# Feed-forward heads of a decoder trunk: evacuations ahead of the block sums, sums grouped, a third tile on the un-normed stream

## The chip, the cores and the metric

One Trainium2 chip, one of its cores. The metric is the device time of one execution in microseconds (us), the median of several; a profile of one execution stands beside it. Times inside a profile count from the start of its span.

## The reference, cut to what matters

The program is a decoder trunk of two layers on 512 tokens of width 1024, in fp32. Each layer has two feed-forward half steps, and this is all that the change touches:

```python
def rms_norm(x, g):
    y = x32 * lax.rsqrt(jnp.mean(x32 * x32, axis=-1, keepdims=True) + EPS)
    return (y * g.astype(jnp.float32)).astype(x.dtype)

def swiglu(h, w_gate, w_up, w_down):
    return (jax.nn.silu(h @ w_gate) * (h @ w_up)) @ w_down
...
    for i in range(DEPTH):
        x = x + 0.5 * swiglu(rms_norm(x, g[0]), ffn_w_gate[i, 0], ffn_w_up[i, 0], ffn_w_down[i, 0])
        ...                                   # mixers: gMLP and HGRN2 in layer 0, latent attention in layer 1
        x = x + 0.5 * swiglu(rms_norm(x, g[2]), ffn_w_gate[i, 1], ffn_w_up[i, 1], ffn_w_down[i, 1])
        x = x + per_layer_embedding(rms_norm(x, g[3]), p[i], ple_w_gate[i], ple_w_proj[i], g[4])
```

`w_gate` and `w_up` are 1024 x 2816, `w_down` is 2816 x 1024. The norm is a factor per token, so (x · gain) @ W, scaled per token afterwards, is the same as rms_norm(x) @ W.

## The kernel before, in words

Activations lie transposed: 1024 features are 8 tiles of 128 partitions x 512 tokens, the 2816 hidden features are 22 such tiles. Every fp32 operand is split in two: a high part, a cast on ScalarE (ACT, L115 in `cut`), and a low part, a subtract on VectorE (DVE, L116). A product is three matmuls, high·high, high·low and low·high (L127 to L129 in `mm3`). `weights` loads a block of weights (a `raw` tile), and splits it into a `wh` and a `wl` tile, five of each in rotation; `feat` multiplies one hidden tile of gate or up from eight feature tiles, 24 matmuls of 128x512; a down tile of `down(0, 4)` is 12 such matmuls.

`ffn` runs four times: two layers, two half steps each. Each run begins with a head. Its order in the source:

- The first two hidden tiles (gate and up each) are multiplied from `x`, the split stream with the gain but without the norm. Their `evacuate` scales them on DVE by `rb`, the norm's factor spread over the partitions (L384, L387), takes silu on ACT, multiplies (L388) and cuts.
- `rb` comes from `norm_of` and `along`: four small matmuls (L223, the spread) and a copy on ACT (L237). In the first and third run (arguments `first` and `tail`) the norm is made while the first two tiles run, and comes late; in the second and fourth it is ready early.
- `quarters` (L321 to L324) makes block differences of the next weights on DVE.
- `normed` (L275 on DVE, then a cut) makes the normed stream, eight tiles `ns`, once `rb` is there.
- The hidden tiles `m` = 2 and 3, called third and fourth here, are multiplied from the normed stream (`rest`).
- `combine` makes sums and differences of halves of the normed tiles (128x256 adds, L289), four of each, and cuts all eight: the operands of a seven-product block scheme.
- Then the third and fourth tile are evacuated: silu from the accumulator on ACT (L382), multiply (L388), cut.
- `down(0, 4)` multiplies the first four hidden tiles into the stream; four of its eight steps stand here, each 12 matmuls and one DVE row that adds to `x` (L448).
- Then the rest: `gate(p)` and `up(p)` call `seven`, seven products (L348 to L350) of 12 matmuls of 128x256 each, weights split as before, with further down steps between.

The engines' orders aren't written by hand. A scheduler merges the source into one order for each engine when the program is built; at run time each engine goes through its own list, and stands where a row waits. Accumulators are named `ps` and `pb`, split tiles `big`, scratch `tmp`.

Of the kernel before, what the change touches and what calls it, by code (L numbers as in the profile page):

```python
# [9 lines left out]
F32R = mybir.dt.float32r  # L10
# [8 lines left out]
KD = DM // P  # L19
# [34 lines left out]
class Net:  # L54
# [228 lines left out]
    def combine(self, ns):  # L283
        V = self.nc.vector
        lo, hi = slice(0, T // 2), slice(T // 2, T)
        self.xc = [{} for _ in range(KD // 2)]

        def add(o, x, y, op):
            V.tensor_tensor(out=o, in0=x, in1=y, op=op)  # L289

        for i, d in enumerate(self.xc):
            d["x11"] = self.halves(ns[2 * i][1])[0]
            d["x12"], d["x22"] = self.halves(ns[2 * i + 1][1])
        sums = []
        for i, d in enumerate(self.xc):
            e, o = ns[2 * i][0], ns[2 * i + 1][0]
            s = self.big()
            add(s[:, lo], e[:, hi], o[:, hi], ALU.add)
            add(s[:, hi], s[:, lo], e[:, lo], ALU.subtract)
            c = self.big(F32R), self.big(F32R)  # L300
            self.cut(*c, s)
            d["s1"], d["s2"] = self.halves(c)
            sums.append(s)
        for i, d in enumerate(self.xc):
            e, o = ns[2 * i][0], ns[2 * i + 1][0]
            s = self.big()
            add(s[:, lo], e[:, lo], e[:, hi], ALU.subtract)
            add(s[:, hi], o[:, lo], sums[i][:, hi], ALU.subtract)
            c = self.big(F32R), self.big(F32R)
            self.cut(*c, s)  # L310
            d["s3"], d["s4"] = self.halves(c)

    def quarters(self, src):
# [57 lines left out]
    def ffn(self, i, f, g_next, embedding=False, tail=None, first=None):  # L371
# [3 lines left out]
        x = self.xs  # L375
        w = a["w_g0"][i, f]
        act = []

        def evacuate(gps, ups, rb=None):
            t, u = self.tmp(), ups  # L380
            if rb is None:
                nc.scalar.activation(out=t, in_=gps, func=AF.Silu)  # L382
            else:
                V.tensor_tensor(out=t, in0=gps, in1=rb, op=ALU.mult)  # L384
                nc.scalar.activation(out=t, in_=t, func=AF.Silu)
                u = self.tmp()
                V.tensor_tensor(out=u, in0=ups, in1=rb, op=ALU.mult)  # L387
            V.tensor_tensor(out=t, in0=u, in1=t, op=ALU.mult)  # L388
            h, l = self.big(F32R), self.big(F32R)
            self.cut(h, l, t)  # L390
            act.append((h, l))
# [29 lines left out]
        if rb is None:  # L421
            rb = self.along(r)
# [2 lines left out]
        evacuate(*pss[:2], rb)  # L425
        evacuate(*pss[2:], rb)
        xn = [c for _, c in ns]
        rest = [self.feat(w[m, n], xn) for m in (2, 3) for n in range(2)]
        self.combine(ns)
        ns = None  # L430
        evacuate(*rest[:2])
        evacuate(*rest[2:])
        gates = {}

        def gate(p):
# [40 lines left out]
        for m in range(3):  # L476
# [3 lines left out]
            for k in range(4):  # L480
                s = slice(k * P, (k + 1) * P)
                self.mm3(pss[m], wh[:, s], wl[:, s], *act[k0 + k], k == 0, False)
        for m in range(3):
            wh, wl, _ = next(early[m])
            for k in range(2):
                s = slice(k * P, (k + 1) * P)
# [927 lines left out]
```

## Time and profile before

| | us |
|---|---|
| median of three runs | 2053.76 |
| lowest and highest | 2048.27, 2054.41 |
| the profiled execution, its own time | 2051.09 |
| its span | 2049.2 |

| engine | busy share of the span |
|---|---|
| PE (TensorE matmuls) | 96% |
| DVE | 76% |
| ACT | 48% |

The chain of work that ended last goes through PE for 84% of the span and through DVE for 10%. The mean granted clock of PE over the span is 0.984 of full. The span is the time from the first to the last instruction that the profile shows; the execution's own time is 1.9 longer.

How to read it: an engine takes its rows in order, so a wait of one row holds all rows behind it. For a stretch the windows view gives each engine's busy time and the granted clock; the timeline gives the starts, and in square brackets the idle time before a row and what ended it. Matmuls are pipelined, so their starts, not their durations, tell the pace. The rows that count stand further below.

### The profile page before, as it was taken

What the parts mean: (1) busy time and instruction counts of PE and PEld (TensorE: products, weight loads), DVE (VectorE), ACT (ScalarE), POOL (GpSimd) and SP (SyncE); (2) the same over time, 40 slices, a digit from 0 to 9 for tenths busy, and PEclk for the clock granted to TensorE, in tenths of its full rate; (3) what the DMA queues carried; (4) which work ended last, traced back from release to release, by engine and by line L of the source; (5) the groups of instructions that cost most, each with busy time, mean ns of one, the idle gap of its engine ahead of it and who ended that gap; (6) DMA issues with size and microseconds to landing.
All of it is one profiled execution on the core that took longest, in us unless ns stands there. A gap on an engine that the chain in (4) does not pass through costs nothing.

```text
span 2049.2 us, 32390 instructions
## 1 busy us (share of the span) xinstructions
PE 1969.0 (96%) x12324; PEld 1761.1 (86%) x12324; DVE 1550.6 (76%) x3047; ACT 992.1 (48%) x1852; POOL 86.4 (4%) x94
## 2 busy tenths in 40 slices
PE   8899999989999999999987999999899999999997
PEld 6799999868887999998976999998777879999996
DVE  7787777677468778777788877775876688778776
ACT  5454445423344554455544544454654455444463
POOL 0000000220000000000000000001420000000001
PEclk9999999999999999999999999999999999999999
DMA  5233333322122233334322333333111222333342
GB/s 174 71 100 103 114 93 104 93 83 70 44 92 94 83 113 93 100 118 124 118 88 67 104 100 116 95 104 97 48 33 35 88 86 91 113 93 98 114 139 88
DMA packets 68571, 193.68 MB, mean 95 GB/s; under 512 B 7744, under 2 KB 10304, under 8 KB 68416
## 3 DMA queue, kind: packets, MB, share of 16 engines
q1 hardware_dynamic: 68416, 191.63, 29.9%
q8 instruction: 96, 1.57, 0.3%
q14 instruction: 59, 0.48, 0.1%
HBM read 189.50 MB, written 2.10 MB: 93 GB/s over the span
## 4 chain that ended last, share of the span: by engine, by line
PE 84%; DVE 10%; DMA 2%; ACT 2%; issue 1%; POOL 0%; SPq 0%; ACTq 0%; DVEq 0%; POOLq 0%
PE ps L127 13%; PE ps L128 13%; PE ps L129 13%; PE ps L349 6%; PE ps L348 6%; PE ps L350 6%; PE pb L348 5%; PE pb L349 5%; PE pb L350 5%; DMA raw<-in_w_gs 2%; DVE wl L116 1%; DVE big L116 1%; PE ps L165 1%; PE ps L166 1%; PE ps L167 1%
## 5 line engine op out<-in xcount | busy, mean ns | idle before, releaser
L115 ACT CAST wh<-raw 128x512 fp32r<-128x512 f32 (+2 forms) x637 | 384.9, 607 | 494.6 <-PE ps L128 167.0
L116 DVE TENSOR_TENSOR wl<-raw,wh 128x512 fp32r<-128x512 f32 (+1 forms) x605 | 406.3, 676 | 201.1 <-ACT wh L115 196.2
L127 PE MATMUL ps<-big,wh 128*128 128x512 f32 (+2 forms) x1376 | 519.2, 382 | 36.6 <-ACT big L115 28.0
L129 PE MATMUL ps<-big,wl 128*128 128x512 f32 (+2 forms) x1376 | 521.3, 380 | 10.2 <-DVE wl L116 10.0
L128 PE MATMUL ps<-big,wh 128*128 128x512 f32 (+2 forms) x1376 | 521.9, 380 | 0.5 <-DVE big L116 0.3
L127 PEld LDWEIGHTS ps<-big,wh 128*128 128x128 f32 (+1 forms) x1376 | 261.1, 190 | 84.9 <-ACT big L115 33.0
L350 PE MATMUL ps<-big,wl 128*128 128x256 f32 x1152 | 326.0, 283 | 0.0
L349 PE MATMUL ps<-big,wh 128*128 128x256 f32 x1152 | 326.0, 283 | 0.0
L348 PE MATMUL ps<-big,wh 128*128 128x256 f32 x1152 | 325.7, 283 | 0.0
L129 PEld LDWEIGHTS ps<-big,wl 128*128 128x128 f32 (+1 forms) x1376 | 261.5, 190 | 59.0 <-DVE wl L116 13.6
L128 PEld LDWEIGHTS ps<-big,wh 128*128 128x128 f32 (+1 forms) x1376 | 262.1, 190 | 49.2 <-DVE big L116 3.3
L115 ACT CAST wh<-tmp 128x512 fp32r<-128x512 f32 x288 | 178.6, 620 | 245.7 <-PE ps L128 118.3
L348 PE MATMUL pb<-big,wh 128*128 128x256 f32 x864 | 246.9, 286 | 1.4 <-DVE big L353 1.1
L349 PE MATMUL pb<-big,wh 128*128 128x256 f32 x864 | 244.4, 283 | 0.0
L350 PE MATMUL pb<-big,wl 128*128 128x256 f32 x864 | 244.3, 283 | 0.0
L348 PEld LDWEIGHTS ps<-big,wh 128*128 128x128 f32 x1152 | 220.9, 192 | 2.7
L349 PEld LDWEIGHTS ps<-big,wh 128*128 128x128 f32 x1152 | 220.9, 192 | 2.7
L350 PEld LDWEIGHTS ps<-big,wl 128*128 128x128 f32 x1152 | 220.9, 192 | 0.0
L116 DVE TENSOR_TENSOR wl<-tmp,wh 128x512 fp32r<-128x512 f32 x288 | 194.6, 684 | 11.0 <-ACT wh L115 9.8
L348 PEld LDWEIGHTS pb<-big,wh 128*128 128x128 f32 x864 | 164.9, 191 | 13.8 <-DVE big L353 13.0
L349 PEld LDWEIGHTS pb<-big,wh 128*128 128x128 f32 x864 | 165.2, 191 | 0.0
L350 PEld LDWEIGHTS pb<-big,wl 128*128 128x128 f32 x864 | 165.0, 191 | 0.0
(271 smaller groups left out, 2593.9 us busy)
## 6 DMA issues: line engine op xcount, KB each, us to landing
raw<-in_w_gs SPq DMA_DIRECT2D x144, 512.0 KB, 4.3
raw<-in_w_dn SPq DMA_DIRECT2D x128, 256.0 KB, 2.7
raw<-in_w_pg SPq DMA_DIRECT2D x28, 512.0 KB, 3.3
raw<-in_w_dn SPq DMA_DIRECT2D x32, 384.0 KB, 3.4
raw<-in_w_ei SPq DMA_DIRECT2D x24, 512.0 KB, 3.6
raw<-in_w_g SPq DMA_DIRECT2D x20, 512.0 KB, 3.5
raw<-in_w_g SPq DMA_DIRECT2D x24, 256.0 KB, 2.7
raw<-in_w_eo SPq DMA_DIRECT2D x8, 512.0 KB, 3.2
```

What stands on the lines that cost most here:

```text
L115: self.nc.scalar.copy(out=h, in_=src)
L116: (eng or self.nc.vector).tensor_tensor(out=l, in0=src, in1=h.bitcast(F32), op=ALU.subtract)
L127: mm(ps, wh, xh, start=first, stop=False)
L128: mm(ps, wh, xl, start=False, stop=False)
L129: mm(ps, wl, xh, start=False, stop=last)
L165: mm(o, x[0][:, t], wh, start=first, stop=False)
L166: mm(o, x[0][:, t], wl, start=False, stop=False)
L167: mm(o, x[1][:, t], wh, start=False, stop=last)
L348: mm(banks[bank], h[:, s], xh, start=new and i == 0, stop=False, **kw)
L349: mm(banks[bank], h[:, s], xl, start=False, stop=False, **kw)
L350: mm(banks[bank], l[:, s], xh, start=False, stop=i == KD // 2 - 1, **kw)
```

## The change

In `ffn`, the tiles `m` = 2 and 3 are each evacuated right behind their products in the source, ahead of `combine` instead of behind it. In the first and third run (`first` or `tail`) the third tile (`m` = 2) is multiplied from the un-normed `x` and scaled by `rb` in its evacuation, like the first two; the fourth, and both in the other two runs, stay on the normed stream. In `combine` all four sums come first, then the four cuts of sums with the differences between them, then the four cuts of differences; before, each sum and each difference was cut at once. Lines behind the edits shift by three or four: L384, L387 and L388 are L387, L390 and L391, and L448 is L452.

```diff
--- before.py
+++ after.py
@@ -292,22 +292,25 @@
             d["x11"] = self.halves(ns[2 * i][1])[0]
             d["x12"], d["x22"] = self.halves(ns[2 * i + 1][1])
         sums = []
-        for i, d in enumerate(self.xc):
+        for i in range(KD // 2):
             e, o = ns[2 * i][0], ns[2 * i + 1][0]
             s = self.big()
             add(s[:, lo], e[:, hi], o[:, hi], ALU.add)
             add(s[:, hi], s[:, lo], e[:, lo], ALU.subtract)
-            c = self.big(F32R), self.big(F32R)
-            self.cut(*c, s)
-            d["s1"], d["s2"] = self.halves(c)
             sums.append(s)
+        diffs = []
         for i, d in enumerate(self.xc):
             e, o = ns[2 * i][0], ns[2 * i + 1][0]
+            c = self.big(F32R), self.big(F32R)
+            self.cut(*c, sums[i])
+            d["s1"], d["s2"] = self.halves(c)
             s = self.big()
             add(s[:, lo], e[:, lo], e[:, hi], ALU.subtract)
             add(s[:, hi], o[:, lo], sums[i][:, hi], ALU.subtract)
+            diffs.append(s)
+        for i, d in enumerate(self.xc):
             c = self.big(F32R), self.big(F32R)
-            self.cut(*c, s)
+            self.cut(*c, diffs[i])
             d["s3"], d["s4"] = self.halves(c)
 
     def quarters(self, src):
@@ -425,11 +428,12 @@
         evacuate(*pss[:2], rb)
         evacuate(*pss[2:], rb)
         xn = [c for _, c in ns]
-        rest = [self.feat(w[m, n], xn) for m in (2, 3) for n in range(2)]
+        for m in (2, 3):
+
+            late = m == 2 and (first or tail)
+            evacuate(*[self.feat(w[m, n], x if late else xn) for n in range(2)], rb if late else None)
         self.combine(ns)
         ns = None
-        evacuate(*rest[:2])
-        evacuate(*rest[2:])
         gates = {}
 
         def gate(p):
```

The number of matmuls stays as it was. DVE has 3035 rows where it had 3029 in the merged lists. The lists of POOL and of the sync queue, which issues the loads, are unchanged. In the lists below `big`, `tmp`, `wl` and `wh` are tiles as above, and the numbers in names tell tiles apart; those of one program aren't those of the other.

PE in the first run's head, behind the norm's spread, before: the third tile's first matmuls take the first normed tile (`big_339`, `big_340`).

```order
L129 MATMUL pb_95<-big_272,wl_225 128x512
L223 MATMUL pb_320<-cst,ty_294 128x128 x4
L127 MATMUL ps_406<-big_339,wh_409 128x512
L127 MATMUL ps_441<-big_339,wh_444 128x512
L127 MATMUL ps_476<-big_339,wh_479 128x512
L128 MATMUL ps_406<-big_340,wh_409 128x512
L129 MATMUL ps_406<-big_339,wl_410 128x512
```

The same place now, with the un-normed tiles `big_88`, `big_89` and `big_133`.

```order
L129 MATMUL pb_95<-big_272,wl_225 128x512
L223 MATMUL pb_320<-cst,ty_294 128x128 x4
L127 MATMUL ps_406<-big_88,wh_409 128x512
L128 MATMUL ps_406<-big_89,wh_409 128x512
L129 MATMUL ps_406<-big_88,wl_410 128x512
L127 MATMUL ps_406<-big_133,wh_409 128x512
```

Behind the spread stand now matmuls on tiles that were there for the first two tiles already.

DVE in the same head, from the last splits of `combine` to the adds of the down steps, before: the low parts of the third and fourth activation (`big_606`, `big_613`) stand behind the last split (`big_599`).

```order
L116 TENSOR_TENSOR big_592<-big_588,big_591 128x512
L289 TENSOR_TENSOR big_595<-big_374 128x256
L289 TENSOR_TENSOR big_595<-big_380,big_567 128x256
L116 TENSOR_TENSOR big_599<-big_595,big_598 128x512
L116 TENSOR_TENSOR big_606<-tmp_602,big_605 128x512
L116 TENSOR_TENSOR big_613<-tmp_609,big_612 128x512
L323 TENSOR_TENSOR tmp_850<-raw_844,tmp_848 128x512
L324 TENSOR_TENSOR tmp_849<-raw_844,raw_843 128x512
L448 SCALAR_TENSOR_TENSOR x<-ps_616,x 128x512
```

DVE now, where the fourth tile is multiplied (L391): its low part (`big_560`) stands ahead of the first add of `combine`.

```order
L391 TENSOR_TENSOR tmp_556<-ps_521,tmp_556 128x512
L116 TENSOR_TENSOR big_483<-tmp_476,big_482 128x512
L116 TENSOR_TENSOR wl_683<-raw_680,wh_682 128x512
L116 TENSOR_TENSOR big_560<-tmp_556,big_559 128x512
L289 TENSOR_TENSOR big_563<-big_338,big_344 128x256
L289 TENSOR_TENSOR big_566<-big_350,big_356 128x256
```

And DVE at the end of `combine` now: the first product's low weight part (`wl_703`, of `raw_326`) stands behind the last split (`big_616`); before, that part stood amid the sums, ahead of the last sum's split.

```order
L116 TENSOR_TENSOR big_604<-big_579,big_603 128x512
L452 SCALAR_TENSOR_TENSOR x<-ps_639,x 128x512
L116 TENSOR_TENSOR big_608<-big_586,big_607 128x512
L452 SCALAR_TENSOR_TENSOR x<-ps_659,x 128x512
L116 TENSOR_TENSOR big_612<-big_593,big_611 128x512
L452 SCALAR_TENSOR_TENSOR x<-ps_679,x 128x512
L116 TENSOR_TENSOR big_616<-big_600,big_615 128x512
L116 TENSOR_TENSOR wl_703<-raw_326,wh_702 128x512
```

What has moved is the whole `combine`, with the adds to `x` strewn in: from ahead of the activations' cuts to behind them, and from behind the first product's weight part to ahead of it. ACT's list follows: its casts of differences (`big_607`, `big_611`, `big_615`) stand behind the cast of a product's weights (`wh_771`).

```order
L115 CAST big_603<-big_579 128x512
L115 CAST wh_771<-tmp_332 128x512
L115 CAST big_607<-big_586 128x512
L115 CAST big_611<-big_593 128x512
L115 CAST big_615<-big_600 128x512
```

In the third run's head the scheduler also moves some 37 small DVE rows of the latent attention's angles (L954 to L996), which stood in the head, to places among the seven-product blocks behind it.

## Rows read from the trace of the kernel before

**Rows 1.** The page, first part: busy us, share of the span, instructions.

```profile
PE 1969.0 (96%) x12324; PEld 1761.1 (86%) x12324; DVE 1550.6 (76%) x3047; ACT 992.1 (48%) x1852; POOL 86.4 (4%) x94
```

**Rows 2.** PE's waits: us in total, times, longest.

```profile
PE ps L127 <- ACT big L115: 28.0, 6, 10.1
```

**Rows 3.** Timeline of PE, first head: start, us, instruction, [idle before, its releaser].

```profile
31.77 0.60 PE L223 MATMUL pb<-cst,ty 128*128 128x128 f32 x4
35.20 0.99 PE L127 MATMUL ps<-big,wh 128*128 128x512 f32 x3 [2.83 <-ACT big L115]
...
59.66 0.39 PE L128 MATMUL ps<-big,wh 128*128 128x512 f32 x1
...
64.64 0.39 PE L129 MATMUL ps<-big,wl 128*128 128x512 f32 x1
73.82 0.80 PE L127 MATMUL ps<-big,wh 128*128 128x512 f32 x1 [8.79 <-ACT big L115]
...
82.64 0.28 PE L348 MATMUL ps<-big,wh 128*128 128x256 f32 x1
82.76 0.28 PE L349 MATMUL ps<-big,wh 128*128 128x256 f32 x1
```

**Rows 4.** Windows: us, busy of PE, PEld, DVE, ACT, POOL, PEclk, DMA share, GB/s.

```profile
28.00:83.00 55.00, 43.20 (x174) 33.78 (x172) 44.53 (x91) 26.09 (x44) 0.00 (x0) 0.88 0.20 58
35.00:40.00 5.00, 4.64 (x13) 3.41 (x14) 5.00 (x10) 3.74 (x6) 0.00 (x0) 0.66 0.16 48
83.00:386.00 303.00, 302.76 (x2039) 279.23 (x2038) 228.29 (x394) 150.68 (x280) 5.17 (x4) 1.00 0.34 103
```

**Rows 5.** Timeline of DVE in the first head.

```profile
33.75 0.75 DVE L275 SCALAR_TENSOR_TENSOR big<-x,par,rb 128x512 f32<-128x512 f32 x1
34.41 0.69 DVE L384 TENSOR_TENSOR tmp<-ps,rb 128x512 f32<-128x512 f32 x1
...
65.10 0.69 DVE L116 TENSOR_TENSOR big<-big,big 128x512 fp32r<-128x512 f32 x1 [0.69 <-ACT big L115]
65.71 0.42 DVE L289 TENSOR_TENSOR big<-big 128x256 f32<-128x256 f32 x1
66.04 0.42 DVE L289 TENSOR_TENSOR big<-big,big 128x256 f32<-128x256 f32 x1
67.14 0.69 DVE L116 TENSOR_TENSOR big<-big,big 128x512 fp32r<-128x512 f32 x1 [0.68 <-ACT big L115]
```

**Rows 6.** Timeline of PE in the third head.

```profile
1060.99 0.98 PE L127 MATMUL ps<-big,wh 128*128 128x512 f32 x3 [2.11 <-ACT big L115]
...
1089.68 0.39 PE L129 MATMUL ps<-big,wl 128*128 128x512 f32 x1
1100.13 1.22 PE L127 MATMUL ps<-big,wh 128*128 128x512 f32 x2 [10.06 <-ACT big L115]
...
1107.77 0.28 PE L348 MATMUL ps<-big,wh 128*128 128x256 f32 x1
```

**Rows 7.** Windows of the third head and of the products behind it.

```profile
1060.00:1108.00 48.00, 36.58 (x146) 28.12 (x147) 46.45 (x113) 22.06 (x39) 0.00 (x0) 0.89 0.16 50
1108.00:1430.00 322.00, 321.74 (x2125) 294.51 (x2124) 240.06 (x418) 161.41 (x298) 5.83 (x6) 1.00 0.33 101
```

**Rows 8.** Timeline of DVE in the third head.

```profile
1059.53 0.75 DVE L275 SCALAR_TENSOR_TENSOR big<-x,par,rb 128x512 f32<-128x512 f32 x1 [2.03 <-ACT rb L237]
...
1094.56 0.28 DVE L980 SCALAR_TENSOR_TENSOR sm<-sm,sm 128x128 f32<-128x128 f32 x1
1094.76 0.28 DVE L978 SCALAR_TENSOR_TENSOR sm<-sm,sm 128x128 f32<-128x128 f32 x1
```

**Rows 9.** Timeline of PE in the second head.

```profile
662.42 0.39 PE L129 MATMUL ps<-big,wl 128*128 128x512 f32 x1
664.80 0.97 PE L127 MATMUL ps<-big,wh 128*128 128x512 f32 x3 [2.00 <-ACT big L115]
...
670.40 0.28 PE L348 MATMUL ps<-big,wh 128*128 128x256 f32 x1
```

## The prediction

> **What bounds the kernel now.** I read the page's first part, then what the tensor engine waits for, then its order of time in the four feed-forward heads, then the same stretches by engine. PE is busy for 96% of the span and DVE for 76% [rows 1], so time can come only out of PE's idle stretches and out of stretches at the lower clock. The list of PE's waits has one entry far above the rest: first-term matmuls (L127) waiting for a high part that ACT cut into a `big` tile, 28.0 us in six waits, the longest 10.1 [rows 2]. Those six lie in the heads of the four feed-forward blocks, where the change is; I call the heads 1 to 4 in order of time. In head 1 PE ends the norm's spread at about 32.1, starts the third tile at 35.20 after an idle of 2.83, ends the first half of the first down products at 64.64 + 0.23 = 64.87 (22 steps from 59.66 to 64.64 make 0.227 a matmul), and stands 8.79 until 73.82 [rows 3]. Head 3 has the same shape: 2.11 before 1060.99 and 10.06 before 1100.13 [rows 6]. Heads 2 and 4, whose norm is early, have one wait each: 2.00 before 664.80 in head 2 [rows 9], and in head 4 what remains of the 28.0, 2.2. After the heads PE has no room left: 302.76 busy of 303 between 83 and 386, with DVE at 228.29 [rows 4]. A head that ends sooner therefore moves everything behind it by as much.
>
> What DVE does in the long wait is the point. From 65.10 on each split of a sum (L116) starts after 0.69 of waiting for ACT, and the next split comes 2.04 later: add, cast on ACT, subtract, one block at a time [rows 5]. The cut of the third tile's activation stands behind all of that on DVE and ACT. It is order, not data, that makes PE wait.
>
> The clock is part of the bill. Between 35 and 40, after the idle of 2.83, the granted clock is 0.66 of full, a mix of its two levels, 2.4 and 1.2 GHz; that is 5.0 x 0.34 = 1.7 lost [rows 4]; the 24 matmuls from 73.82 to 82.64 take 8.82 where 24 x 0.227 = 5.45 would do, so 3.4 are lost after the idle of 8.79 [rows 3]. In head 3 the like stretch takes 1107.77 - 1100.13 = 7.64, 2.2 lost [rows 6]. In head 2 it takes 670.40 - 664.80 = 5.60: an idle of 2.00 lost nothing [rows 9].
>
> **The change part by part.** Prices of DVE rows are distances between starts of queued rows, which are less than durations: a 128x512 subtract 0.61 (65.10 to 65.71), `normed` 0.66 (33.75 to 34.41), a 128x256 add 0.33 (65.71 to 66.04) [rows 5]. I use 0.60 for every 128x512 row but `normed`, 0.67 and 0.34.
>
> *Third tile from the un-normed stream, heads 1 and 3.* Its 48 matmuls need no norm, so they start behind the spread, at 32.1 instead of 35.20, at full clock, and end at 32.1 + 48 x 0.227 = 43.0. The fourth tile still needs the normed stream, and DVE makes that: the 32 rows from the first `normed` at 33.75 to the last normed low part, now with the third tile's two scaling products and one multiply among them, are 8 x 0.67 + 23 x 0.60 + 0.2 = 19.4, so 53.2. Eight matmuls stand behind that last part, 1.8, with some 0.2 to start: the fourth tile ends at 55.2. Before it ended at 64.87 - 24 x 0.227 = 59.4 [rows 3]. That is 4.2 gained. Four products are added on DVE in the whole program (two in each late head); they lie inside the 19.4.
>
> *Evacuations ahead of the combine, sums grouped.* Before, the first product started 82.64 - 59.4 = 23.2 after the fourth tile. Now PE goes on without a wait through all 48 down matmuls, to 55.2 + 10.9 = 66.1, since the last activation's parts stand ahead of the combine. What is late next is the first product's low weight part, which the order puts behind the whole combine on DVE. From the end of the fourth tile: 0.2 to start, one multiply, two cuts and a down-weight cut (4 x 0.60 = 2.4), eight adds of the sums (2.7), then eight splits, eight adds of the differences and four adds to x (4.8 + 2.7 + 2.4 = 9.9), then that low part (0.7): 15.9, so 71.1. Two product matmuls of 0.12 (82.64 to 82.76 [rows 3]) run before it is needed, so PE waits from 66.3 to 71.1, 4.8, and the product stands as if started at 70.9. Gain against 82.64: 11.7.
>
> The new idle of 4.8 lies between 2.83, which cost 1.7, and 8.79 and 10.06, which cost 3.4 and 2.2. I take the mean of the three, 2.4, with 0 and 3.4 as ends. Head 1: -11.7 + 2.4 = **-9.3**. The Trainium skill (TensorE: Matmul & The Clock Gate, section HAM oscillation) holds that a long enough idle of PE throws it back to its lower clock until it has worked again; by that rule the new idle is not free and the sum stays, and this trace agrees at 2.83 and above, and shows no fall at 2.00.
>
> *Head 3.* The spread is pushed behind four matmuls of the third tile, so the first `normed` row comes 4 x 0.227 = 0.9 later than 1059.53 [rows 8]; 32 rows of the same kinds, 19.4, bring the last normed part to 1079.8 and the fourth tile's end to 1081.8, instead of 1089.91 - 5.45 = 1084.5 [rows 6]. The cuts of the first activations are still queued on DVE then: eight of 0.60 and two small ones, 5.1, to 1084.9. After that 2.7 + 9.9 + 0.7 give 1098.2 for the low part of the second product, which here is the late one (the first one's stands ahead of the combine). The first product stands as if started at 1098.2 - 0.24 - 1.44 = 1096.5 (1.44 is twelve matmuls of 0.12) instead of 1107.77: -11.3, and with 2.4 for the clock **-8.9**. Some 37 small rows of the odd layer's angles, 0.20 each between starts [rows 8], 7.6 together, stood largely in this head (113 DVE rows against 91 in head 1 [rows 4, 7]) and now stand among the products behind it. There DVE is busy for 240.06 of 322 [rows 7], so I take **+0.5**, from 0 to 2.
>
> *Heads 2 and 4.* No third-tile change; the wait of 2.00 goes. But DVE now has nothing from about 647 to 657, since the combine stands behind the fourth tile's multiply, which needs PE. From the fourth tile's end at 662.65 - 5.45 = 657.2: multiply, one weight cut, one activation cut with 0.2 to start 2.0, adds of the sums 2.7, seven splits, eight adds and four adds to x 4.2 + 2.7 + 2.4 = 9.3, the second product's low part 0.7: 671.9. PE is there at 657.2 + 10.9 + 1.44 + 0.24 = 669.8 and waits 2.1. The first product stands as if at 670.2 instead of 670.40: **-0.2** each. An idle of 2.1 is nearest to the 2.00 that cost no clock; the other end is 1.7 each.
>
> Matmuls are as many as before. The orders of the sync queue and of POOL are unchanged, so no transfer moves past another.
>
> **How the numbers follow.** -9.3 - 8.9 + 0.5 - 0.4 = -18.1. Against the profiled execution, 2051.1, that is 2033.0; its median of three stands 2.7 higher, and I put the forecast a little up, at **2034**. About 0.3%, 6 us, is what a measurement of this kernel tells from no change.
>
> **Rivals.**
> No clock is lost in the new idles: -11.7 - 11.3 - 0.4 + 0.5 = -22.9, 2028 against the profiled execution and 2031 against the median. For it: some idles fall without a loss (2.00). Against: 2.83 lost 1.7. Chance 0.13.
> ACT holds half the splits. In ACT's order the casts of the differences stand behind casts of product weights, which wait for a weight tile that PE frees only at the end of each down product. By my times the last of them comes at 66.1, about 1 before DVE asks for the parts behind it; if PE is later than that, four splits a head fall back to the old 2.04 instead of 0.60 + 0.68 = 1.28, 3.0 a head, 12 in all: 2046. Chance 0.13, about half of it within 0.3%.
> The third tile isn't early, because its weights' cuts hold it: the fourth tile then ends at 59.4 and only the second gain is left, 11.7 - 4.2 - 2.4 = 5.1 in heads 1 and 3: 2041. Against: those weights' rows stand ahead of the first `normed` on DVE. Chance 0.05.
> Slower: all eight splits of every head stay a ping-pong at 2.04. That is 8 x 0.76 = 6.1 a head, 24 in four, and it lengthens the idles of heads 2 and 4 past 2.83, where each loses 1.7 of clock: 2034 + 24 + 3 = 2061. It decides from 18.1 / 32 = 0.57 a split on. Against it: four finished sums lie ready for ACT before DVE needs the first cast. Chance 0.05. The Trainium skill (VectorE: DVE Perf Modes, section The DRAIN you can't avoid) found a chain of DVE copies equally long with and without a semaphore after each; by that rule regrouping brings nothing, which is this rival. The trace doesn't follow it here: the 0.68 is a wait for another engine.
>
> The forecast itself has 0.64: it holds from 2028 to 2040. The range, **2027 to 2043**, takes in the gain without a clock loss and the late third tile, and leaves out most of the ACT case and the slower one. Faster by over 0.3% (below 2047.6) 0.88, within 0.3% 0.07, slower 0.05.
>
> **What would show it.** Right: no idle before the third tile in heads 1 and 3; the fourth tile's end near 55 and 1082; down products without a gap; then one idle of 3 to 5 before a product, put down to DVE's `wl`, with a stretch of half clock behind it; in heads 2 and 4 about 2 at the second product. DVE's splits 1.3 apart. Wrong: idles before products as long as those removed, splits 2 apart waiting for ACT, a third tile that starts at 35, or PE gaps among the products behind head 3.

## The result, and the profile after

| | before | after |
|---|---|---|
| median, us | 2051.20 (four runs, 2048.27 to 2054.41) | 2027.51 (four runs, 2023.85 to 2030.27) |
| ratio after / before | | 0.9883, 95% interval 0.9858 to 0.9908 |
| profiled execution, span | 2049.2 | 2026.0 |
| mean granted clock of PE | 0.984 | 0.988 |

The change gains 23.7 us. PE's waits for a high part that ACT cuts, 28.0 us in [rows 2], are down to 0.8; two new kinds of wait at the first products take their place. PE's waits after, in us, times and longest:

```profile
PE ps L353 <- DVE wl L116: 7.0, 4, 3.2
PE ps L351 <- DVE x L452: 2.0, 2, 1.4
...
PE ps L127 <- ACT big L115: 0.8, 2, 0.6
```

Head 1 on PE after, beside [rows 3] (start, us, instruction, idle before and its releaser):

```profile
31.14 0.60 PE L223 MATMUL pb<-cst,ty 128*128 128x128 f32 x4
31.50 0.48 PE L127 MATMUL ps<-big,wh 128*128 128x512 f32 x1
...
65.45 0.39 PE L129 MATMUL ps<-big,wl 128*128 128x512 f32 x1
65.68 0.28 PE L351 MATMUL ps<-big,wh 128*128 128x256 f32 x1
...
66.95 0.38 PE L351 MATMUL ps<-big,wh 128*128 128x256 f32 x1 [0.63 <-DVE x L452]
67.17 0.28 PE L352 MATMUL ps<-big,wh 128*128 128x256 f32 x1
70.63 0.58 PE L353 MATMUL ps<-big,wl 128*128 128x256 f32 x1 [3.18 <-DVE wl L116]
71.01 0.41 PE L351 MATMUL ps<-big,wh 128*128 128x256 f32 x1
```

The third tile starts behind the spread without a wait, the down products run without a gap to 65.68, and the first wait is for a product's low weight part. DVE in the same head:

```profile
54.82 0.69 DVE L391 TENSOR_TENSOR tmp<-ps,tmp 128x512 f32<-128x512 f32 x1 [0.33 <-ACT big L115]
...
57.24 2.76 DVE L289 TENSOR_TENSOR big<-big,big 128x256 f32<-128x256 f32 x8
59.92 0.68 DVE L116 TENSOR_TENSOR big<-big,big 128x512 fp32r<-128x512 f32 x1
...
69.29 0.68 DVE L116 TENSOR_TENSOR big<-big,big 128x512 fp32r<-128x512 f32 x1
69.89 1.28 DVE L116 TENSOR_TENSOR wl<-raw,wh 128x512 fp32r<-128x512 f32 x2
```

From 54.82 to 71.09 DVE goes from row to row without a wait: the fourth tile's multiply, the eight adds of the sums, eight splits between 59.92 and 69.29, then the low parts of the first two products. PE stands behind that list. The windows view (us, busy of PE, PEld, DVE, ACT, POOL, PEclk, DMA share, GB/s) shows full clock where [rows 4] had 0.66, and what the new idle costs:

```profile
35.00:40.00 5.00, 5.00 (x24) 4.13 (x23) 4.91 (x9) 4.35 (x8) 0.00 (x0) 1.00 0.06 23
69.00:76.00 7.00, 5.37 (x25) 5.37 (x26) 5.30 (x10) 1.51 (x3) 0.00 (x0) 0.51 0.14 37
```

Between 69 and 76 the granted clock is at the lower of the two levels (1.2 GHz), and from 70.63 on PE works at it: product matmuls start 0.21 apart instead of 0.12. About 2.6 are lost there.

Where the 23.2 of the span went, from starts of rows that stand in both traces, outside the heads:

| stretch | before | after | earlier by | gained in it |
|---|---|---|---|---|
| first spread (L223), ahead of head 1's edits | 31.77 | 31.14 | 0.63 | 0.6 |
| low weight part (L129) behind head 1 | 423.35 | 412.78 | 10.57 | 9.9 |
| L129 ahead of head 2 | 638.75 | 627.84 | 10.91 | 0.3 |
| sum of squares (L216) ahead of head 3 | 1052.53 | 1040.13 | 12.40 | 1.5 |
| L165, mixer behind head 3 | 1449.91 | 1427.73 | 22.18 | 9.8 |
| L129 ahead of head 4 | 1648.87 | 1625.35 | 23.52 | 1.3 |
| L127 behind the last feed-forward block | 2031.72 | 2008.47 | 23.25 | -0.3 |

The 0.6 comes before anything that the change touches. Of the 1.3, 1.0 appears between 1540.40 and 1648.87: before, PE's granted clock was 0.57 between 1541 and 1545, after, it was 1.00 at the like place (1518 to 1523), though PE's wait ahead of it was as long (2.15 and 2.14, see the last section). So about 21 of the 23.2 lie where the change is, and some 2 are differences of one execution from another.

### The profile page after: what moved, and what is told of

Its sections match the earlier page's. It is cut to its first block, busy times and chain, and to the rows that moved or that the text cites. A ratio compares the mean times of both kernels' runs of the same rounds, so it can differ in the third digit from the quotient of the medians.

```text
span 2026.0 us, 32400 instructions
## 1 busy us (share of the span) xinstructions
PE 1963.4 (97%) x12324; PEld 1758.6 (87%) x12324; DVE 1545.8 (76%) x3051; ACT 990.1 (49%) x1852; POOL 86.5 (4%) x94
## 4 chain that ended last, share of the span: by engine, by line
PE 85%; DVE 10%; ACT 2%; DMA 1%; issue 1%; POOL 0%; SPq 0%; ACTq 0%; DVEq 0%; POOLq 0%
PE ps L129 13%; PE ps L127 13%; PE ps L128 13%; PE ps L353 7%; PE ps L352 7%; PE ps L351 7%; PE pb L351 5%; PE pb L353 5%; PE pb L352 5%; DVE wl L116 1%; DVE big L116 1%; PE ps L165 1%; PE ps L166 1%; PE ps L167 1%; PE pb L899 1%
## 5 line engine op out<-in xcount | busy, mean ns | idle before, releaser
L116 DVE TENSOR_TENSOR wl<-raw,wh 128x512 fp32r<-128x512 f32 (+1 forms) x605 | 405.4, 675 | 197.1 <-ACT wh L115 194.2
L127 PE MATMUL ps<-big,wh 128*128 128x512 f32 (+2 forms) x1376 | 520.0, 379 | 9.3 <-ACT wh L115 6.2
L129 PE MATMUL ps<-big,wl 128*128 128x512 f32 (+2 forms) x1376 | 518.7, 378 | 10.2 <-DVE wl L116 10.0
L129 PEld LDWEIGHTS ps<-big,wl 128*128 128x128 f32 (+1 forms) x1376 | 259.8, 189 | 58.3 <-DVE wl L116 13.7
L127 PEld LDWEIGHTS ps<-big,wh 128*128 128x128 f32 (+1 forms) x1376 | 260.1, 189 | 55.0 <-ACT wh L115 6.6
L116 DVE TENSOR_TENSOR wl<-tmp,wh 128x512 fp32r<-128x512 f32 x288 | 193.8, 682 | 7.4 <-ACT wh L115 6.3
```

What stands on the lines that cost most here:

```text
L116: (eng or self.nc.vector).tensor_tensor(out=l, in0=src, in1=h.bitcast(F32), op=ALU.subtract)
L127: mm(ps, wh, xh, start=first, stop=False)
L129: mm(ps, wl, xh, start=False, stop=last)
```

## The experiments

Each kernel is timed against the kernel before; ratios carry their 95% interval. Diffs are against the changed kernel where nothing else is said.

**The third tile alone** (against the kernel before).

```diff
-        rest = [self.feat(w[m, n], xn) for m in (2, 3) for n in range(2)]
+        late = bool(first or tail)
+        rest = [self.feat(w[m, n], x if late and m == 2 else xn) for m in (2, 3) for n in range(2)]
         self.combine(ns)
         ns = None
-        evacuate(*rest[:2])
+        evacuate(*rest[:2], rb if late else None)
         evacuate(*rest[2:])
```

> The third tile from the un-normed stream alone: evacuations of the third and fourth tile stay behind the combine, sums and differences stay cut one by one. Theory of the prediction (the three edits lean on each other): the fourth tile ends about 4 us earlier in heads 1 and 3, but the activation that PE waits for is cut behind the combine, and the combine's last split on DVE is no earlier; PE waits 13 and 15 us instead of 8.8 and 10.1, so 2050 to 2054, no change. Rival (the earlier tile pays by itself): 4.2 in each of two heads and no half clock at its start, 2 x 5, so about 2041.

Measured: 2049.30, ratio 0.9996 (0.9986 to 1.0005). No change. PE in head 1:

```profile
61.67 0.39 PE L129 MATMUL ps<-big,wl 128*128 128x512 f32 x1
75.78 0.80 PE L127 MATMUL ps<-big,wh 128*128 128x512 f32 x1 [13.73 <-ACT big L115]
```

All rows of this trace lie 1.8 later than before from the start on (the spread is at 33.59, in [rows 3] at 31.77). Counted from the spread, PE gets to the wait 4.8 sooner (28.3 against 33.1) and leaves it at the same time (42.2 against 42.1): what the third tile gained, its idle of 2.83 and the half clock behind it, has moved into the wait for the combine, 13.73 instead of 8.79. Edited alone, the part that removes a visible wait is worth nothing.

**The evacuations alone** (against the kernel before; `combine` as before, third tile from the normed stream).

```diff
-        rest = [self.feat(w[m, n], xn) for m in (2, 3) for n in range(2)]
+        for m in (2, 3):
+            late = False
+            evacuate(*[self.feat(w[m, n], x if late else xn) for n in range(2)], rb if late else None)
         self.combine(ns)
         ns = None
-        evacuate(*rest[:2])
-        evacuate(*rest[2:])
```

> Only the evacuations ahead of the combine; the third tile waits for the norm in heads 1 and 3 as before (2.8 and 2.1), and sums and differences are cut one by one. Theory of the prediction (the splits stay a ping-pong of 2.04, so without the grouping the combine is 16.4 long behind the fourth tile instead of 12.6): products wait 5 to 8 in every head, clock falls again, gain 3 to 8, so 2043 to 2048. Rival (grouping isn't needed, since in this order DVE's list puts the products' weight parts and adds to x into the idle 0.68 between splits): PE waits nowhere over 1 us behind the fourth tile, 16 of idle and 5 of clock gone, so 2029 to 2032.

Measured: 2026.41, ratio 0.9880 (0.9865 to 0.9895), as much as the whole change. Behind the fourth tile no wait in the heads is over 0.6. It is faster than the rival's 2029 to 2032 too. The theory that the grouping is needed falls here.

**The grouping alone** (against the kernel before; `combine` as changed).

> Only the grouping in the combine; evacuations stay behind it, the third tile waits for the norm. Theory of the prediction (eight splits at 1.28 instead of 2.04 end the combine 6 earlier): PE's waits for the activation fall from 8.8 and 10.1 to 2 to 4, the 2.0 and 2.2 of heads 2 and 4 vanish, little half clock, so 2030 to 2036. Rival (regrouping brings nothing by itself, as the rule on chained DVE rows would have it): 2050 to 2054.

Measured: 2032.79, ratio 0.9911 (0.9896 to 0.9926). The six waits of 28.0 shrink to these two lines. The second is the third tile's wait for the norm, as before:

```profile
PE ps L127 <- DVE tmp L391: 5.6, 2, 3.1
...
PE ps L127 <- ACT big L115: 4.9, 2, 2.8
```

There are 1.6 and 1.1 more at a down step's low weight part in heads 1 and 3. With the evacuations left behind it, a shorter combine does help.

**The change without the grouping.** `combine` is that of the kernel before, the rest as changed.

> The change without the grouping: evacuations ahead of the combine and the third tile from the un-normed stream, but sums and differences cut one by one. Theory of the prediction (its slower rival: every split a ping-pong at 2.04, 6.1 more in each of four heads and the clock lost in all): 2040 to 2055. Rival (ungrouped, DVE's list takes the products' weight parts into the gaps between splits, so no product waits for the whole combine): no wait over 1 us in the heads, no half clock there, some 4 better than the change, 2021 to 2026.

Measured: 2021.17 (2020.37 to 2022.38), ratio 0.9853 (0.9839 to 0.9868). The prediction's slower rival would have made this version the slow one; it is faster than the change. DVE in head 1 shows why:

```profile
59.67 0.69 DVE L116 TENSOR_TENSOR big<-big,big 128x512 fp32r<-128x512 f32 x1
60.28 0.42 DVE L289 TENSOR_TENSOR big<-big,big 128x256 f32<-128x256 f32 x1
60.61 0.69 DVE L449 SCALAR_TENSOR_TENSOR x<-ps,x 128x512 f32<-128x512 f32 x1
61.21 0.42 DVE L289 TENSOR_TENSOR big<-big,big 128x256 f32<-128x256 f32 x1
61.54 0.69 DVE L116 TENSOR_TENSOR wl<-tmp,wh 128x512 fp32r<-128x512 f32 x1
62.14 0.69 DVE L321 TENSOR_TENSOR tmp<-raw 128x512 f32<-128x512 f32 x1
62.74 0.69 DVE L116 TENSOR_TENSOR big<-big,big 128x512 fp32r<-128x512 f32 x1
```

Splits of the sums (L116 of `big`) are 3.07 apart, farther than before, but there is no idle in brackets: an add to x, a weight part and a block difference stand between them. The scheduler fills ACT's round trip, and PE is in the products from 65.66 on, while the combine's last split comes at 79.28. PE's only wait over 0.6 between 60 and 83 is 1.64 for a sum at 76.18, and the clock holds:

```profile
60.00:80.00 20.00, 17.91 (x111) 15.83 (x110) 19.70 (x40) 9.99 (x17) 0.00 (x0) 1.00 0.24 75
```

**Both once more, on one chip.**

> The changed kernel once more, beside the version without grouping on one chip. All theories: 2024 to 2030 as in its first runs, with 3 us of wait for a low weight part in head 1 and half clock behind it.

> The version without grouping once more, beside the changed kernel on one chip. Theory (the grouping costs 4 to 7 in all, from waits for weight parts and adds to x behind the unbroken combine, and the clock they cost): 2020 to 2023, 4 to 7 below the changed kernel, intervals apart. Rival (the difference of the first runs was one of chips and days): within 2 of the changed kernel.

Measured: the change 2028.06 (2023.69 to 2028.68), ratio 0.9877 (0.9862 to 0.9892); without grouping 2021.93 (2021.30 to 2022.63), ratio 0.9852 (0.9837 to 0.9866). The two intervals touch, by 0.0004, but over all runs of both none of the one, eight from 2020.4 to 2022.6, lies among the other's eight, from 2023.7 to 2030.3. The grouping costs about 6. By the rows of the table above, the two traces of the change gain 9.9 and 10.2 in head 1 and 9.8 and 9.7 in head 3, those without grouping 13.9 and 13.8, and 13.1 and 12.6; heads 2 and 4 differ by 0.7 at most. Of the 3 in head 3, 1.7 is a fall of the clock at the norm (from 1041 on in the change), which both traces of the change have and neither of those without grouping; whether the grouping has a part in that stays open.

**The change without its third tile** (`late = False`): evacuations and grouping.

> The change without the third tile from the un-normed stream: evacuations first and sums grouped, the third tile waits for the norm in heads 1 and 3. If the grouping costs by itself (4 to 6, as the step from the change to its version without grouping gave): 2030 to 2033, with the waits of 2.8 and 2.1 before the third tile and 1 to 3 at a product's low weight part in each head. Rival (grouping costs only because the earlier tile brings PE to the combine sooner): about 2026, as with the evacuations alone.

Measured: 2032.99, ratio 0.9909 (0.9888 to 0.9929). Against the evacuations alone (0.9865 to 0.9895) the grouping loses some 6 here too, so it costs by itself and not because of the earlier tile. The third tile gains 5.5 on top of this version, and 5 on top of the evacuations alone.

**The first two weights ahead of the combine.**

```diff
+        pre = [self.split(w_) for w_ in ws[:2]]
         self.combine(ns)
...
-            gates[p] = self.seven(ws if p == 2 else self.quarters(a["w_gs"][i, f, p - 2, 0]))
+            gates[p] = self.seven(ws, pre) if p == 2 else self.seven(self.quarters(a["w_gs"][i, f, p - 2, 0]))
```

`split` allocates a `wh` and a `wl` and cuts; `seven` takes the given pairs for its first products.

> The change, with the first two products' weights of the first gate split ahead of the combine in the source. Theory (the wait in the grouped version is for the low weight part, which DVE makes behind eight splits): the first two products, 2.9 us of PE's work, run while DVE is at the combine, the wait shrinks below 2 and the clock stays up, 2018 to 2022. Rival (the adds to x, which give the down products' accumulators free, stand among the same splits, and a product needs such an accumulator): PE waits about as long for an add to x, 3 in head 1, and the clock falls there as before, 2024 to 2028.

Measured: 2023.70 (2023.25 to 2029.40), ratio 0.9871 (0.9852 to 0.9890), which doesn't tell it from the change and lies between its two forecasts. The traced execution is the slowest of four, 2029.40, the others lie between 2023.25 and 2023.92; it has a stretch at half clock outside the heads (0.51 from 1009 to 1016) that the change's trace doesn't have. What it shows of the heads is the kind of the wait. PE in head 1, and the clock there:

```profile
67.72 0.58 PE L355 MATMUL ps<-big,wh 128*128 128x256 f32 x1 [2.68 <-DVE x L457]
...
66.00:74.00 8.00, 6.21 (x28) 5.92 (x29) 5.95 (x12) 2.63 (x6) 0.00 (x0) 0.57 0.12 33
```

The wait for a product's weight part is gone, and a wait for an add to x, which frees a `ps` accumulator, is in its place. Two things stand among and behind the splits of the unbroken combine, and PE needs both. The rival of this run holds in head 1 as to the wait; the longest waits of heads 2 and 4 did shrink, from 1.3 to 0.35. Whether the whole gains some us, as the three faster executions would have it, stays open.

**Only the sums grouped**: as the change, but each difference is cut at once.

> The change, with the sums grouped as in it, but each difference cut at once, as before. Theory (what costs is one unbroken row of eight splits and 16 adds on DVE; a round trip between differences lets DVE take weight parts and adds to x in between): 2020 to 2024. Rival (grouping the sums alone already puts the weight parts behind): 2026 to 2029.

Measured: 2022.48 (2020.51 to 2024.26), ratio 0.9858 (0.9841 to 0.9876). That is 0.6 to 1.3 above the two medians of the version without grouping: broken up in its second half, the combine costs almost nothing.

**Another order of the seven products**, on the version without grouping: `x11`, `x12`, `x22` first, and the add of the `z` bank behind `plus(o22, "y", o21)`.

> The version without grouping (evacuations first, third tile from the un-normed stream), with the seven products in another order: the three that need no sum or difference (x11, x12, x22) first, the add of the third one's result later. Theory (what is left in the heads are waits of 0.3 to 1.6 of the third and later products for the combine): 4.3 of PE's work cover it, 2 to 3 gained, 2017 to 2020. Rival (those waits are for weights and accumulators in rotation, not for sums): 2020 to 2022, no gain on the version without grouping.

Measured: 2033.07, ratio 0.9912 (0.9896 to 0.9927), 12 slower than without it; neither reading had that. The list of PE's waits names it:

```profile
PE pb L348 <- DVE big L353: 8.2, 8, 1.7
```

In the version without grouping this entry is 0.8 us in two waits. The new order holds in every gate and up, not just the first, and keeps a `pb` accumulator from the third product to the last add, so later products wait for one. The growth of these waits is 7 of the 12. The traced execution also runs at a granted clock of 0.57 from 1011 to 1019, about 3.4 lost, where the version without grouping keeps 1.00; that may be of this execution alone, and what is left stays open.

**Both late tiles from the un-normed stream**, on the version without grouping (`late = bool(first or tail)`).

> The version without grouping, with the fourth tile from the un-normed stream too in heads 1 and 3. Theory of the prediction (the fourth tile ends at about 55 because DVE makes the normed stream then): it ends at 32 + 96 x 0.227 = 53.8 in head 1, but DVE has two more products a head and is what bounds the combine, so later products wait for it by as much: 2020 to 2025, no gain. Rival (PE's earlier end is kept): 2 a head, 2016 to 2018.

Measured: 2023.21 (2019.82 to 2024.36), ratio 0.9855 (0.9839 to 0.9872): no gain. The fourth tile's multiply on DVE comes later, not earlier. First the version with one such tile, then this one:

```profile
54.79 0.69 DVE L388 TENSOR_TENSOR tmp<-ps,tmp 128x512 f32<-128x512 f32 x1 [0.33 <-ACT big L115]
```

```profile
54.76 0.70 DVE L387 TENSOR_TENSOR tmp<-ps,rb 128x512 f32<-128x512 f32 x1
55.36 0.70 DVE L116 TENSOR_TENSOR big<-tmp,big 128x512 fp32r<-128x512 f32 x1
55.96 0.70 DVE L388 TENSOR_TENSOR tmp<-tmp,tmp 128x512 f32<-128x512 f32 x1
```

The tile's second scaling product (L387) stands right ahead of it on a list without idle. DVE bounds the head there, and the time agrees with the theory: two more products on it cost what PE saves.

## Why the prediction was right, and where it was wrong

*The place and the kind of the waits* were right: no idle ahead of the third tile, no gap in the down products (but for 0.26 and 0.22 in head 4), then a wait of a product for DVE's `wl`, with half clock behind it in heads 1 and 3.

*The fourth tile's end.* Predicted 55.2; its multiply starts at 54.82, with the head 0.6 ahead of the old times. DVE's 32 rows were priced right: the first `normed` is at 33.13 and the last normed low part at 52.00, 18.9 against 18.8 by the same prices without that part's own 0.6.

*Head 1.* The low part was forecast for 71.1 and used at 70.63; 4.8 of idle came out as 0.63 + 3.18, since the list lets PE run the first terms of three products ahead of the wait. The clock cost 2.6 against 2.4. Gain 9.9 against 9.3.

*Head 3* was mis-sized: 9.8 against 8.9 - 0.5. Some 37 small rows among the products cost almost nothing (waits of 0.3), and PE waited 1.38, 0.41, 0.29 and 1.17, 3.25 in all, where its terms make one wait of 3.8; and the clock cost 1.7 (4.00 at 0.57), not 2.4.

```profile
1081.26 0.38 PE L351 MATMUL ps<-big,wh 128*128 128x256 f32 x1 [1.38 <-DVE x L452]
...
1083.60 0.39 PE L351 MATMUL pb<-big,wh 128*128 128x256 f32 x1 [0.41 <-ACT wh L115]
1084.39 0.39 PE L351 MATMUL ps<-big,wh 128*128 128x256 f32 x1 [0.29 <-ACT big L359]
...
1086.06 0.48 PE L353 MATMUL ps<-big,wl 128*128 128x256 f32 x1 [1.17 <-DVE wl L116]
...
1086.00:1090.00 4.00, 3.94 (x20) 3.94 (x21) 3.24 (x6) 0.62 (x1) 0.00 (x0) 0.57 0.00 0
```

*Heads 2 and 4.* The trade of a wait of 2 for one at the second product was right, 1.35 instead of 2.1. Head 2 gained 1.5 against 0.2; head 4, with the same two waits, lost 0.3. What the traces name between the two: three waits of 0.2 to 0.4 among head 2's products before, which are gone after, and two new ones of 0.26 and 0.22 in the first down product of head 4 (1646.32, 1647.04), for the two parts of the fourth activation. That is some 1.3 of 1.8; the rest stays open.

*The total.* 18.1 was forecast, about 21 measured in the heads' stretches and 23.7 between the medians: too small by 0.6, 1.4 and 1.3 in heads 1, 3 and 2, too large by 0.5 in head 4, and short of some 2 that are not of the change. The median lies at the low end of the range, 2027 to 2043. It is also what the rival without a clock loss forecast, 2028; that is chance, since the clock did fall, for 2.6 in head 1 and 1.7 in head 3.

*The step that failed* is the worth of the grouping. The prediction took the 2.04 between splits of [rows 5] for what an ungrouped combine costs anywhere, and built its slower rival on it. That distance held because nothing else stood on DVE's list at that place. With the evacuations ahead, adds to x and weight parts are ready by then, and the scheduler puts them into the gaps. Ungrouped is faster by 6. The total of the prediction came out near all the same, because it gave head 1's second gain, 11.7 - 4.2 = 7.5, to the evacuations and the grouping together. The evacuations alone gain 10.8 in head 1 and 9.8 in head 3 (by the rows of the table above), as much as the change; the grouping and the third tile about cancel. The rule that it cited from the Trainium skill (VectorE: DVE Perf Modes, The DRAIN you can't avoid) was read as a reason why regrouping might bring nothing. The grouping alone brought 17, so that reading fails; the wait that it shortened was for ACT.

*The ACT rival* didn't come about: in head 1 the last three casts of differences ran from 66.23, behind a weight cast at 65.71, and DVE took each of them without a wait.

## What to carry to other kernels

A wait that is visible on the bounding engine may be only the first of two: taking away the third tile's wait alone moved the time into the next one. Grouping like operations shortens a chain and lengthens the time in which its engine does nothing else; before grouping, see which other results of that engine are due in that time, weight parts and freed accumulators here. The version without grouping, 2021 to 2022, is the one to keep; with the sums alone grouped the time, 2022.5, is not told apart from it.

## What the runs showed of the hardware

The length of the single longest idle of PE doesn't tell whether the clock falls. Idles of 2.00 and 2.24 in heads 2 and 4 before cost no clock [rows 9], and the prediction leaned on that. But in head 3 after the change four idles of 0.3 to 1.4 with little work between them, from 1081.26 to 1086.06, were followed by a granted clock of 0.57 between 1086 and 1090, so mostly the lower level; the change's second trace has the same waits and the same 0.57. And the same idle can go either way. In the third tile alone the one of head 4 is 2.00 again, and here the clock fell:

```profile
1671.85 1.21 PE L127 MATMUL ps<-big,wh 128*128 128x512 f32 x4 [2.00 <-ACT big L115]
...
1673.00:1677.00 4.00, 4.00 (x12) 3.10 (x11) 2.73 (x6) 0.93 (x2) 0.00 (x0) 0.57 0.00 0
```

A mixer behind head 3 has a wait of 2.14 or 2.15 in all thirteen traces of this case, at code that no version touches. In six of them the clock falls behind it, in seven it doesn't. Before, and after:

```profile
1540.40 0.70 PE L1201 MATMUL pb<-big,big 128*128 128x256 f32 x2 [2.15 <-ACT big L1209]
1541.00:1545.00 4.00, 4.00 (x21) 3.82 (x20) 3.09 (x17) 1.98 (x6) 0.47 (x1) 0.57 0.00 2
```

```profile
1517.91 0.70 PE L1205 MATMUL pb<-big,big 128*128 128x256 f32 x2 [2.14 <-ACT big L1213]
1518.00:1523.00 5.00, 5.00 (x32) 4.03 (x33) 4.80 (x22) 3.25 (x9) 0.98 (x2) 1.00 0.02 6
```

The first of these two is in the trace that the prediction read. Each of these falls costs 1.7 (4.00 at 0.57), so a forecast that puts an idle of some 2 us at no loss, or at a sure loss, can be off by that much at each place.

Nor does the view have to show an idle. In a mixer between heads 1 and 2 PE runs 32 matmuls of one output column each, busy throughout by the profile, and the clock falls; it does so in all thirteen traces. Before:

```profile
538.51 4.59 PE L216 MATMUL pb<-cst,big 128*128 128x1 f32 x32
...
541.00:548.00 7.00, 7.00 (x35) 6.08 (x35) 3.33 (x10) 0.62 (x1) 0.00 (x0) 0.51 0.00 0
```
